# Interleaving the gate and up accumulations of a feed-forward pair, matmul by matmul, in a float32 two-block kernel

## Chip, cores and metric

The kernel runs on one NeuronCore of a Trainium2 chip. The metric is the time of one execution on the device in microseconds, as the median of several runs; lower is better.

## What is computed

Two residual blocks follow each other on 512 tokens of width 1024, all in float32. Each block is a half-weighted feed-forward, a mixer and a second half-weighted feed-forward. The mixer of the first block is a retention with a pooled branch, that of the second a gated delta rule with a short convolution. Most of the arithmetic is in the four feed-forwards:

```python
D_MODEL, SEQ, D_FF = 1024, 512, 2816

def rmsnorm(x, g):
    xf = x.astype(jnp.float32)
    y = xf * lax.rsqrt(jnp.mean(xf * xf, axis=-1, keepdims=True) + NORM_EPS)
    return (y * g.astype(jnp.float32)).astype(x.dtype)

def swiglu_ffn(x, w_in, w_out):
    gate, up = jnp.split(x @ w_in, 2, axis=-1)
    return (jax.nn.silu(gate) * up) @ w_out

# in each block
h = h + 0.5 * swiglu_ffn(rmsnorm(h, norm_ffn1), ffn1_w_in, ffn1_w_out)
...
h = h + 0.5 * swiglu_ffn(rmsnorm(h, norm_ffn2), ffn2_w_in, ffn2_w_out)
```

## The kernel before, in words

Activations lie transposed, with the channels on the 128 partitions and the 512 tokens along the free dimension. A row of 128 channels is one tile of 128x512; the residual has KD = 8 rows, the inner width of a feed-forward KF = 22.

Every float32 operand of a large product is split into two parts, `hi` and `lo` for activations, `wh` and `wl` for weights (`split_into`, L200: ScalarE writes the high part at L202, then VectorE the rest at L203). A product is then three matmuls (`mm3`, L217): `wh` with `hi` (L218), `wh` with `lo` (L219), `wl` with `hi` (L220). All three add to one PSUM tile.

A tile of weights is loaded and split by `weights` (L208): SyncE starts a DMA into a raw tile `wr`, ScalarE makes `wh` from it and VectorE `wl`. Each of the three kinds has three buffers, used in turn: weight tile number i takes the buffers of tile i-3.

`projs` (L226) multiplies the rows `xs` with some weight tiles, each into a PSUM tile `ps` of its own with the tag `mm`. In the feed-forward (`ffn`, L348) it is called once for each of the 22 pairs f: weight tile 2f gives the gate, 2f+1 the up part. It takes the 8 rows of x for the gate (24 matmuls), then the 8 rows for the up part (24 matmuls). The `late` form, used for f = 0, does the last row of x after the others; `steps` are pieces of the norm that are run between. After the matmuls of pair f come, in the program, the steps that empty pair f-1: VectorE multiplies the gate sums with the norm's scale (L363), ScalarE applies SiLU (L364), VectorE scales the up sums (L366), multiplies both (L368), and the product is split again. There are six PSUM buffers, so three pairs. After the pairs the same helper `weights` feeds the second product with `w_out`, 66 matmuls into one PSUM tile for each of 8 output rows.

`projs` with two weight tiles is also called in the first mixer (L503) for the two halves of the query and of the key of each of four heads.

The instructions of an engine stand in a fixed order, which a scheduler chooses when the kernel is built. It starts from the order of the program and moves an instruction back where, by its own reckoning of times, its inputs come later than those of others.

Of the kernel before, what the change touches and what calls it, by code (L numbers as in the profile page):

```python
# [16 lines left out]
P = 128  # L17
T = 512
NT = T // P
D = 1024  # L20
# [3 lines left out]
EPS = 1e-6  # L24
# [3 lines left out]
SB = 16  # L28
# [35 lines left out]
def shape_constants():  # L64
    """Tables that follow from the shapes alone."""
    c = np.zeros((P, NCONST), np.float32)
# [43 lines left out]
class Steps:  # L110
    """A generator that is run a step at a time, and what it returns."""

# [32 lines left out]
def tile_blocks(ctx: ExitStack, tc: tile.TileContext, ins, out, stop=None):  # L145
    nc = tc.nc
# [37 lines left out]

# [1 line left out]
    def tmp():  # L186
# [5 lines left out]
    def split(dst_pool, tag, bufs, src, shape=None, scale=None):  # L192
        """src = hi + lo exactly, both of the width that one pass takes."""
        shape = shape or [P, T]
        hi = dst_pool.tile(shape, F32R, name=nm("hi"), tag=tag, bufs=bufs)
        lo = dst_pool.tile(shape, F32R, name=nm("lo"), tag=tag, bufs=bufs)
        split_into(hi, lo, src, scale)
        return hi, lo
# [9 lines left out]
    def weights(src, nk, m):  # L208
        """One stage of weights: [P, nk, m] of them, split on arrival."""
        raw = wp.tile([P, nk, m], F32, name=nm("wr"), tag="wr", bufs=3)  # L210
        nc.sync.dma_start(raw, src)
        wh = wp.tile([P, nk, m], F32R, name=nm("wh"), tag="wh", bufs=3)
        wl = wp.tile([P, nk, m], F32R, name=nm("wl"), tag="wl", bufs=3)
        split_into(wh, wl, raw)
        return wh, wl
# [6 lines left out]
    def proj(psp, src, xs, bufs):  # L222
        """[P outputs, T] of the rows xs through one tile of weights."""
        return projs(psp, [src], xs, bufs)[0]

    def projs(psp, srcs, xs, bufs, steps=(), ws=None, order=None, late=False):  # L226
        """The same through some tiles of weights, a late last row after all others, with steps of something else between."""
        n = len(xs)
        ws = ws or [weights(src, n, P) for src in srcs]
        pss = [psp.tile([P, T], F32, name=nm("ps"), tag="mm", bufs=bufs) for _ in srcs]  # L230
        order = order or range(n)
        for ks in ((order[: n - 1], order[n - 1 :]) if late else (order,)):
            for (wh, wl), ps in zip(ws, pss):
                for k in ks:
                    mm3(ps, wh[:, k, :], wl[:, k, :], *xs[k], k == order[0], k == order[-1])
                if len(ks) > 1 and steps:
                    steps[0].step()
                    steps = steps[1:]
        return pss

    def rsqrt_cols(src, n, scale, eps=EPS):
        """(src * scale + eps) ** -0.5, by Newton steps."""
        v = rp.tile([P, n], F32, name=nm("rv"), tag="rv", bufs=4)
        nc.vector.tensor_scalar(v, src, scale, eps, ALU.mult, ALU.add)
        return newton(v, n)
# [15 lines left out]
    def spread(psp, cols, groups=1):  # L261
        """cols [P tokens, NT, groups] as [P, T]: each group's on its share of the partitions."""
        ps = psp.tile([P, T], F32, name=nm("pb"), tag=SM[0][0], bufs=SM[0][1])
        spread_into(ps, cols, groups)
        return ps
# [8 lines left out]
    def row_sums(psp, parts, of, tag=None):  # L274
        """-1 times the sums over the partitions that each column of `of` takes."""
        tag, bufs = tag or SM[0]
        ps = psp.tile([P, T], F32, name=nm("pr"), tag=tag, bufs=bufs)
        for j, part in enumerate(parts):
            nc.tensor.matmul(ps, of, part, start=(j == 0), stop=(j == 1))
        return ps  # L280

    def rms_rows(psp, src, sq, y, scale, eps):
        """y = (sum * scale + eps) ** -0.5 [P, T] of the sums of src over all partitions, with sq as scratch: from a logarithm, then a Newton step. In steps."""
        parts = [tp.tile([P, T], F32R, name=nm("t"), tag="t", bufs=5) for _ in range(2)]
# [13 lines left out]
    class Prep:  # L298
        """Takes the rows of the residual as they get ready: their split products with a gain,
        and the sums of their squares."""  # L300

# [28 lines left out]
        def scales(self, psp):  # L330
            """1/rms of each token, on all partitions [P, T], in steps; with a second gain also that of the
            normed row times it: 1/sqrt(s2/D + EPS (s1/D + EPS)) of the sums s1, s2 of squares."""
            (acc, sq), rest = self.last[0], self.last[1:]
# [70 lines left out]
    def last_add(d):  # L404
        """The squares of a finished row of the last residual; the row itself gets its gain."""
        sq = stmp()
# [9 lines left out]
    def last_out(psp, op, ps, cols):  # L416
        """The last row, for some tokens, and what depends on it: their norm and output."""
        d, n = KD - 1, (cols.stop - cols.start) // P
# [37 lines left out]
    def mix1(prep, nxt):  # L456
        xs = prep.xs
        w = ins["w_in"]
        with ExitStack() as c:
# [25 lines left out]
            with ExitStack() as c2:  # L485
# [11 lines left out]
                for hd in range(RH):  # L497
# [16 lines left out]
                    qs, ks = qk  # L514
                    # v with tokens on partitions
                    if hd == 0:
# [7 lines left out]
                    for t in range(NT):  # L524
# [9 lines left out]
                        if t in (1, 2) and fin:  # L534
                            fin[t + 1].step()
                    # scores of the tokens up to each chunk's end
                    offs = [0, 512, 896, 1152]
# [104 lines left out]
    def mix2(prep, nxt):  # L642
# [3 lines left out]
        with ExitStack() as c:  # L646
            yp = K.pool(c, nm("yc"))
            yc, os_ = [None] * 4, [None] * GH
            with ExitStack() as c2:
# [46 lines left out]
                def tok_sums(s, n, rhs):  # L696
                    """Sums over partitions of a tile [P, T], as columns [P tokens, NT, n]."""
                    ps = bank([P, NT, n])
# [10 lines left out]

                # b and a, a token per partition  # L710
                sc = Steps(prep.scales(psp))
# [15 lines left out]
                def decays():  # L727
                    """beta and the decays of all heads."""
                    yield LAG["d0"]
# [15 lines left out]
                    nc.vector.tensor_tensor(th(z), ba[:, :, 4:8], hb(vcol("gdn_dt_bias_2", 0, 4)), ALU.add)  # L745
                    # softplus(z) = max(z, 0) + log(1 + e), e = exp(-|z|); log(1 + e) = 2 atanh(e / (2 + e))
                    e_, s_, s2, a_ = ct(16), ct(16), ct(16), ct(16)
# [13 lines left out]
                    yield LAG["d2"]  # L761
                    # sums within a chunk, its last one, and the decays
                    pg = bank([P, 16])
# [26 lines left out]
                def conv(x_, names, i, kw):  # L790
                    """Causal convolution over the tokens of a tile of channels."""
                    nt = 12 if kw == 4 else 4
# [18 lines left out]
                def settle():  # L811
                    """What awaits the last row: the norm, and the rest of b and a."""
                    nonlocal rb
                    ba_rows(range(KD))
                    rb, = sc.result()
                    shorts.append(Steps(decays()))

                def chain(hd, q, k, v):
                    gl, er, dec = decay(hd)
                    bh, egh, gdh = (th(x)[:, :, hd] for x in (beta, eg, gd))  # L820
                    # k and v with tokens on partitions
                    pk = bank()
# [17 lines left out]
                    yield LAG["c1"]  # L840
                    # 1/|k| as columns
                    irk, es = ct(4), ct(4)
# [19 lines left out]
                    yield LAG["c5"]  # L862
                    # the inverse of a unit triangle: blocks of SB by substitution, with the rows of each
                    # block on all its partitions, then two doublings
                    c32 = ep.tile([P, NT, 2 * SB], F32, name=nm("c32"), tag="c32", bufs=2)
# [69 lines left out]
                    yield LAG["c10"]  # L935
                    # the recurrence over chunks, from a state of zeros
                    st = gp.tile([P, P], F32, name=nm("st"), tag="st", bufs=2)
                    po = psp.tile([P, T], F32, name=nm("po"), tag="o", bufs=1)
                    for ci in range(NCH):
# [29 lines left out]
                        yield LAG["r1"]  # L969
                    # the norm of the output, with that of q in it  # L970
                    so = stmp()
# [66 lines left out]
                def tick():  # L1038
                    """After a pass of the projections: one step of what is due, its LAG of passes after the last."""
                    tick.n += 1  # L1040
# [25 lines left out]

# [1 line left out]
    def dump():  # L1068
# [47 lines left out]

# [1 line left out]
def _tiles(w):  # L1118
    """[K, N] as [N/P, P, K/P * P]: each tile of output columns in one run per partition."""
    k, n = w.shape  # L1120
# [5 lines left out]
def _cols(v):  # L1126
    """[..., n * P] as [P, ... * n]."""
    return np.asarray(v).reshape(-1, P).T
# [62 lines left out]
```

## Time and profile before

| | |
|---|---|
| median of 3 runs | 2309.75 us (2309.1 to 2310.97) |
| span of the profiled execution | 2307.3 us |
| the median less that span | 2.45 us |
| TensorE busy | 2272.6 us, 98% of the span |
| weight loads (beside matmuls) | 1863.1 us |
| VectorE busy | 1137.0 us, 49% |
| ScalarE busy | 810.3 us, 35% |
| mean granted TensorE clock | 0.995 of full speed |

No time of the profiled execution as a whole is listed beside its span; the runs' median is 2.45 us above the span, which is taken as what lies around it. TensorE's busy time adds up overlapping matmuls, whose ends are modelled; how fast it goes is read from the distance between the starts of successive matmuls. Idle time of an engine that is not the bottleneck costs nothing.

### The profile page before, as it was taken

How to read it: one execution, taken by the hardware profiler on the slowest of the kernel's cores; microseconds unless marked ns; L12 is line 12 of the kernel's file. 1: busy time of each engine (PE TensorE's matmuls, PEld its weight loads, DVE VectorE, ACT ScalarE, POOL GpSimd, SP SyncE). 2: the span in 40 equal slices, each digit the busy share in tenths (PEclk: the TensorE clock that was granted, in tenths of full speed). 3: DMA queues.
4: the chain of work that ended last, by engine and by line, in shares of the span. 5: the costliest groups of instructions: out<-in, count | busy, mean ns of one | idle time of the engine just before them, and what ended most of it. 6: DMA issues, size and time to landing. Idle time of an engine off the chain costs nothing. (4 is left out here: it accounts for less than half of the span.)

```text
span 2307.3 us, 25697 instructions
## 1 busy us (share of the span) xinstructions
PE 2272.6 (98%) x10476; PEld 1863.1 (81%) x10476; DVE 1137.0 (49%) x1703; ACT 810.3 (35%) x1059; POOL 76.3 (3%) x78
## 2 busy tenths in 40 slices
PE   8999999999999999999999999999999999999998
PEld 6888888888878888888888888887777778888887
DVE  6444434665553444444336444334867655444332
ACT  5232223444432234233235332223534344233221
POOL 1000000000210000000000000000111000000000
PEclk9999999999999999999999999999999999999999
DMA  4333333222233333333333333333211123323332
GB/s 158 92 100 100 92 93 108 87 87 83 74 100 101 91 99 99 99 94 98 94 91 95 98 99 96 90 99 93 65 46 37 47 58 98 101 91 101 94 94 69
DMA packets 61190, 208.34 MB, mean 90 GB/s; under 512 B 6800, under 2 KB 9232, under 8 KB 61072
## 3 DMA queue, kind: packets, MB, share of 16 engines
q1 hardware_dynamic: 58544, 203.48, 28.9%
q10 hardware_dynamic: 2528, 3.21, 0.4%
q8 instruction: 82, 1.34, 0.2%
q14 instruction: 36, 0.29, 0.0%
HBM read 204.57 MB, written 2.10 MB: 90 GB/s over the span
## 5 line engine op out<-in xcount | busy, mean ns | idle before, releaser
L218 PE MATMUL ps<-hi,wh 128*128 128x512 f32 (+1 forms) x2774 | 1082.8, 391 | 6.4 <-ACT wh L202 6.4
L219 PE MATMUL ps<-lo,wh 128*128 128x512 f32 (+1 forms) x2774 | 1082.4, 390 | 0.8 <-DVE lo L206 0.8
L220 PE MATMUL ps<-hi,wl 128*128 128x512 f32 (+1 forms) x2774 | 1082.3, 390 | 0.6 <-DVE wl L203 0.6
L202 ACT ACTIVATE wh<-wr 128x1024 fp32r<-128x1024 f32 (+1 forms) x390 | 406.3, 1042 | 1159.6 <-PE ps L219 630.8
L203 DVE TENSOR_TENSOR wl<-wr,wh 128x1024 fp32r<-128x1024 f32 (+1 forms) x390 | 470.2, 1206 | 341.1 <-ACT wh L202 340.8
L218 PEld LDWEIGHTS ps<-hi,wh 128*128 128x128 f32 x2774 | 521.9, 188 | 119.5 <-ACT wh L202 6.4
L219 PEld LDWEIGHTS ps<-lo,wh 128*128 128x128 f32 x2774 | 521.5, 188 | 115.7 <-DVE lo L206 3.2
L220 PEld LDWEIGHTS ps<-hi,wl 128*128 128x128 f32 x2774 | 521.5, 188 | 114.9 <-DVE wl L203 2.5
L366 DVE TENSOR_TENSOR t<-ps,rb 128x512 f32<-128x512 f32 x88 | 60.7, 690 | 258.6 <-PE ps L220 258.6
L363 DVE TENSOR_TENSOR t<-ps,rb 128x512 f32<-128x512 f32 x88 | 60.8, 690 | 169.9 <-PE ps L220 169.8
L202 ACT ACTIVATE hi<-t 128x512 fp32r<-128x512 f32 x119 | 75.2, 632 | 112.2 <-DVE t L368 62.0
L807 PE MATMUL ps<-hi,wh 128*128 128x512 f32 x224 | 94.4, 422 | 0.4 <-DVE t L1001 0.4
L807 PE MATMUL ps<-hi,wl 128*128 128x512 f32 x224 | 93.3, 416 | 0.0
L807 PE MATMUL ps<-lo,wh 128*128 128x512 f32 x224 | 92.6, 413 | 0.0
L203 DVE TENSOR_TENSOR lo<-t,hi 128x512 fp32r<-128x512 f32 x119 | 83.3, 700 | 5.4 <-ACT hi L202 5.1
L368 DVE TENSOR_TENSOR t<-t,t 128x512 f32<-128x512 f32 x88 | 60.8, 691 | 8.2
L364 ACT ACTIVATE t<-t 128x512 f32<-128x512 f32 x88 | 54.2, 616 | 3.4 <-DVE t L363 3.3
L377 DVE SCALAR_TENSOR_TENSOR h<-ps,h 128x512 f32<-128x512 f32 x31 | 21.4, 691 | 64.4 <-PE ps L220 64.4
L807 PEld LDWEIGHTS ps<-hi,wh 128*128 128x128 f32 x224 | 42.9, 191 | 8.2 <-issue 1.0
L807 PEld LDWEIGHTS ps<-hi,wl 128*128 128x128 f32 x224 | 42.4, 189 | 8.3 <-issue 0.9
L807 PEld LDWEIGHTS ps<-lo,wh 128*128 128x128 f32 x224 | 43.1, 192 | 6.9 <-issue 0.2
L530 PE MATMUL pv<-wh,hi 128*128 128x256 f32 x128 | 36.3, 284 | 0.0
(292 smaller groups left out, 1362.1 us busy)
## 6 DMA issues: line engine op xcount, KB each, us to landing
wr<-in_ffn_w_in SPq DMA_DIRECT2D x176, 512.0 KB, 3.5
wr<-in_ffn_w_out SPq DMA_DIRECT2D x64, 512.0 KB, 3.6
wr<-in_w_in SPq DMA_DIRECT2D x48, 512.0 KB, 3.5
wr<-in_w_mix_in SPq DMA_DIRECT2D x28, 512.0 KB, 3.5
wr<-in_ffn_w_out SPq DMA_DIRECT2D x32, 384.0 KB, 3.1
wr<-in_w_v SPq DMA_DIRECT2D x8, 512.0 KB, 3.8
wr<-in_w_ret_up SPq DMA_DIRECT2D x8, 512.0 KB, 3.4
wr<-in_w_pool_up SPq DMA_DIRECT2D x8, 512.0 KB, 3.5
```

The costliest lines, as they stand in the source:

```text
L202: nc.scalar.activation(hi, src, AF.Copy)
L203: nc.vector.tensor_tensor(lo, src, hi.bitcast(F32), ALU.subtract)
L218: nc.tensor.matmul(ps, lh, rh, start=start, stop=False)
L219: nc.tensor.matmul(ps, lh, rl, start=False, stop=False)
L220: nc.tensor.matmul(ps, ll, rh, start=False, stop=stop)
L363: nc.vector.tensor_tensor(g, pg, rb, ALU.mult)
L364: nc.scalar.activation(g, g, AF.Silu)
L366: nc.vector.tensor_tensor(u, pu, rb, ALU.mult)
L368: nc.vector.tensor_tensor(m, g, u, ALU.mult)
L377: nc.vector.scalar_tensor_tensor(h[d], ps, 0.5, h[d], ALU.mult, ALU.add)
L530: nc.tensor.matmul(pv, xh[:, sl], wh[:, k % 4, :], start=(k == 0), stop=False)
L807: nc.tensor.matmul(ps, a[:, k, :], b, start=(k == j == 0), stop=(k == KD - 1 and j == 2))
```

## The change

Where `projs` has more than one weight tile, no late row and no steps, it now goes through the rows k of x, for each through the three kinds of matmul, and for each of these through the weight tiles: gate and up alternate. The matmuls of such pairs have line 237; later lines are 7 higher (L363 is L370, L366 is L373, L368 is L375). The rest of the diff takes out comments and docstrings.

```diff
         order = order or range(n)
+        if len(pss) > 1 and not late and not steps:
+            for k in order:
+                for j in range(3):
+                    for (wh, wl), ps in zip(ws, pss):
+                        a = (wh, wh, wl)[j][:, k, :]
+                        nc.tensor.matmul(ps, a, xs[k][j == 1], start=(k == order[0] and j == 0), stop=(k == order[-1] and j == 2))
+            return pss
         for ks in ((order[: n - 1], order[n - 1 :]) if late else (order,)):
             for (wh, wl), ps in zip(ws, pss):
                 for k in ks:
```

The form applies to 83 pairs of the feed-forwards (all but f = 0 of each, and f = 1 of the first, which has steps) and to the key pair of each of the four heads. The number of matmuls is the same.

TensorE, in the first feed-forward, before: the end of the gate and the start of the up part of one pair. ps_984 and ps_985 are the gate and up sums of the pair, wh_974 and wl_975 the gate's weights, wh_980 and wl_981 the up part's; hi and lo are rows of x.

```order
L218 MATMUL ps_984<-hi_146,wh_974 128x512
L219 MATMUL ps_984<-lo_147,wh_974 128x512
L220 MATMUL ps_984<-hi_146,wl_975 128x512
L218 MATMUL ps_985<-hi_105,wh_980 128x512 [waits Activation_49]
L219 MATMUL ps_985<-lo_106,wh_980 128x512
L220 MATMUL ps_985<-hi_105,wl_981 128x512 [waits DVE_49]
```

The last use of the gate's wh_974 stands 25 matmuls before the pair's end.

TensorE, the same place in the changed kernel: the end of that pair, and then the start of the next one, whose sums are ps_1057 and ps_1058, with wh_1047 and wl_1048 for the gate and wh_1053 and wl_1054 for the up part. wh_1053 and wl_1054 take the buffers of wh_974 and wl_975.

```order
L237 MATMUL ps_984<-lo_147,wh_974 128x512
L237 MATMUL ps_985<-lo_147,wh_980 128x512
L237 MATMUL ps_984<-hi_146,wl_975 128x512
L237 MATMUL ps_985<-hi_146,wl_981 128x512
L237 MATMUL ps_1057<-hi_105,wh_1047 128x512 [waits Activation_49]
L237 MATMUL ps_1057<-lo_106,wh_1047 128x512
L237 MATMUL ps_1057<-hi_105,wl_1048 128x512 [waits DVE_49]
L237 MATMUL ps_1058<-hi_105,wh_1053 128x512 [waits Activation_49]
L237 MATMUL ps_1058<-lo_106,wh_1053 128x512
```

```order
L237 MATMUL ps_1057<-hi_110,wh_1047 128x512
L237 MATMUL ps_1057<-lo_111,wh_1047 128x512
L237 MATMUL ps_1057<-hi_110,wl_1048 128x512
L237 MATMUL ps_1058<-hi_105,wl_1054 128x512 [waits DVE_49]
L237 MATMUL ps_1058<-hi_110,wh_1053 128x512
```

The second fence follows directly on the first. The scheduler has moved the first up matmuls back by a few places; from the 13th matmul of a pair on, gate and up alternate strictly. The last use of wh_974 now stands 7 matmuls before the first use of wh_1053 and 12 before the first use of wl_1054.

VectorE around the same pair, in the changed kernel: the emptying of the gate sums ps_984 (L370) and of the up sums ps_985 (L373), with the weights' low parts between.

```order
L370 TENSOR_TENSOR t_1107<-ps_984,rb_267 128x512 [waits PE_49]
L203 TENSOR_TENSOR wl_1054<-wr_1051,wh_1053 128x1024 [waits DMAHW3_49,Activation_49]
L373 TENSOR_TENSOR t_1110<-ps_985,rb_267 128x512 [waits PE_49]
L203 TENSOR_TENSOR wl_1121<-wr_1118,wh_1120 128x1024 [waits DMAHW4_49,Activation_49]
L375 TENSOR_TENSOR t_1112<-t_1107,t_1110 128x512 [waits DVE_49,Activation_49]
```

Before, the order of the first three was the same, and wl_1121 stood behind the product L368. On ScalarE wh_1053 stands behind the previous pair's steps as before, and wh_1120 now directly behind it.

## Rows read from the trace of the kernel before

**Rows 1.** The page: the span, and two lines of its 40 slices in tenths.
```profile
span 2307.3 us, 25697 instructions
PE   8999999999999999999999999999999999999998
PEclk9999999999999999999999999999999999999999
```

**Rows 2.** Timeline of TensorE, 100 to 124 us: start us, us, engine, line, operation.
```profile
99.73 0.39 PE L218 MATMUL ps<-hi,wh 128*128 128x512 f32 x1
99.96 0.39 PE L219 MATMUL ps<-lo,wh 128*128 128x512 f32 x1
100.19 0.39 PE L220 MATMUL ps<-hi,wl 128*128 128x512 f32 x1
100.42 0.39 PE L218 MATMUL ps<-hi,wh 128*128 128x512 f32 x1
...
105.40 0.39 PE L219 MATMUL ps<-lo,wh 128*128 128x512 f32 x1
105.63 0.39 PE L220 MATMUL ps<-hi,wl 128*128 128x512 f32 x1
...
123.99 0.39 PE L220 MATMUL ps<-hi,wl 128*128 128x512 f32 x1
```

**Rows 3.** Timeline of VectorE, 100 to 124 us; in brackets the idle time before.
```profile
100.61 0.69 DVE L366 TENSOR_TENSOR t<-ps,rb 128x512 f32<-128x512 f32 x1 [3.30 <-PE ps L220]
101.41 0.69 DVE L368 TENSOR_TENSOR t<-t,t 128x512 f32<-128x512 f32 x1
102.02 1.22 DVE L203 TENSOR_TENSOR wl<-wr,wh 128x1024 fp32r<-128x1024 f32 x1
...
106.06 0.69 DVE L363 TENSOR_TENSOR t<-ps,rb 128x512 f32<-128x512 f32 x1 [2.21 <-PE ps L220]
106.97 1.22 DVE L203 TENSOR_TENSOR wl<-wr,wh 128x1024 fp32r<-128x1024 f32 x1 [0.23 <-ACT wh L202]
```

**Rows 4.** Timeline of ScalarE, 100 to 124 us.
```profile
105.88 1.06 ACT L202 ACTIVATE wh<-wr 128x1024 fp32r<-128x1024 f32 x1 [3.11 <-PE ps L219]
```

**Rows 5.** Timeline of TensorE, product with w_out, 299.7 to 311.9 us: first and last.
```profile
299.40 0.40 PE L220 MATMUL ps<-hi,wl 128*128 128x512 f32 x1
...
311.77 0.40 PE L219 MATMUL ps<-lo,wh 128*128 128x512 f32 x1
```

**Rows 6.** Timelines of ScalarE and of weight loads, start of the kernel: TensorE's wait.
```profile
5.30 1.06 ACT L202 ACTIVATE wh<-wr 128x1024 fp32r<-128x1024 f32 x1 [0.67 <-DMA wr<-in_ffn_w_in]
...
6.40 0.29 PEld L218 LDWEIGHTS ps<-hi,wh 128*128 128x128 f32 x1 [6.40 <-ACT wh L202]
```

**Rows 7.** Timeline of all engines, 656 to 660 us: a wait of TensorE on VectorE.
```profile
655.92 0.69 DVE L203 TENSOR_TENSOR lo<-t,hi 128x512 fp32r<-128x512 f32 x1 [0.70 <-ACT hi L202]
...
656.67 0.19 PEld L219 LDWEIGHTS pm<-lo,wh 128*128 128x128 f32 x1 [0.54 <-DVE lo L203]
...
656.78 0.19 PEld L220 LDWEIGHTS pm<-hi,wl 128*128 128x128 f32 x1
...
659.07 0.50 PE L218 MATMUL pm<-hi,wh 128*128 128x512 f32 x1 [1.66 <-DVE lo L206]
```

**Rows 8.** Timeline of TensorE, matmuls of 256 columns, 404.7 to 407.9 us: first and last.
```profile
404.51 0.28 PE L530 MATMUL pv<-wh,hi 128*128 128x256 f32 x1
...
407.87 0.28 PE L531 MATMUL pv<-wl,hi 128*128 128x256 f32 x1
```

**Rows 9.** Timeline of TensorE, 1660.6 to 1664.2 us, in the second mixer.
```profile
1661.09 0.63 PE L807 MATMUL ps<-hi,wh 128*128 128x512 f32 x1
1661.52 1.91 PE L271 MATMUL pg<-cst,c 128*128 128x128 f32 x8
```

**Rows 10.** Stretches: PE, PEld, DVE, ACT, POOL busy (instructions), granted clock, DMA share, GB/s.
```profile
650.00:660.00 10.00, 8.12 (x34) 5.91 (x33) 8.07 (x12) 4.02 (x6) 2.17 (x2) 1.00 0.44 113
...
1661.00:1664.00 3.00, 3.00 (x15) 2.81 (x13) 2.69 (x7) 2.88 (x6) 0.00 (x0) 0.50 0.35 78
```

## The prediction

> **What bounds the kernel now.** I read the page first: TensorE has no slice below 0.8 and full clock in all 40 [rows 1]. So time is matmuls times the distance of their starts, plus gaps. The next view is the timeline of TensorE inside a feed-forward. From 99.73 to 123.99 us there are 107 distances in 24.26 us, 0.2267 us each, with no gap [rows 2]. A pair of 48 takes 10.88 us.
>
> The same view answers the change's question, since it holds a change of bank every 24 matmuls. The matmul at 100.19 is the last of an up part: VectorE starts to empty it at 100.61 [rows 3]. The next, at 100.42, is the first of a gate, in another bank. Their distance is 0.23; the 24 distances from 100.19 to 105.63, this one among them, average 0.2267, and the 23 without it 0.2265 [rows 2]. A switch of bank gains nothing that can be seen. Nor does it matter whether successive matmuls share weights: L218 to L219 does, L219 to L220 does not, and both distances are 0.23.
>
> Then the timelines of ScalarE and VectorE for what prepares weights. The split of a tile starts when the last matmul that reads the buffer's former tile is done: L219 at 105.40, ScalarE at 105.88, 0.48 later [rows 2, 4]. VectorE's part starts 1.09 after ScalarE's and takes 1.22 [rows 3, 4]. Before the change that is far ahead of need: the up part's buffers come free in the middle of a pair, and 24 matmuls (5.4 us) pass before the pair ends.
>
> **The change, part by part.** *Same count of matmuls, loads and DMAs.* Nothing is added; bank switches rise from 2 to 40 in a pair (counted in the order of the changed kernel), for 87 pairs. Price of a switch: 0, by the distance at 100.42.
>
> *The same x row in two successive matmuls.* The trace has no such pair. Its nearest rows are the two distances that it shows for other operands, 0.2267 in the pairs and 12.37 us over 53, 0.2334, in the product with w_out [rows 2, 5]. Bounds: 0.0067 more for some 20 such successions in 87 pairs, 12 us; below, a gain down to the fixed part worked out under the rivals. I take 0, since operands and buffers are those of the 0.2267 rows.
>
> *Weights needed sooner and released later.* This is the term that counts. The gate's `wh` is now read up to the 45th matmul of its pair, and its buffer is what the next pair's up weights wait for. In the changed order the next up part first reads `wh` 7 matmuls after that release matmul and `wl` 12 after it. Counted from the start of the release matmul:
>
> - due: `wh` at 7 x 0.2267 = 1.587 us, `wl` at 12 x 0.2267 = 2.72 us;
> - `wh` ready: 0.48 (release to ScalarE) + 1.06 (its duration [rows 4]) + 0.04 (6.36 to 6.40, its end to the weight load [rows 6]) = 1.58 us;
> - `wl` ready: 0.48 + 1.09 + 1.22 + 0.06 (656.61 to 656.67 [rows 7]) = 2.85 us;
> - after a wait the weight load is no longer hidden: the next load follows 0.11 after the first (656.67 to 656.78 [rows 7]). So the matmuls run at 1.69 and 2.96.
>
> `wh` is 0.10 late, and `wl` 0.24 late in all (the first delay is inside it). VectorE must be free: its gate evacuation stands directly ahead of `wl`. It starts 0.43 after its last matmul (105.63 to 106.06 [rows 2, 3]), which is two after the release: 0.45 + 0.43 = 0.88. The next operation can follow 0.61 later (101.41 to 102.02 [rows 3]), at 1.49, before `wh` is done at 1.57. So it hides, by 0.08 us; with the 0.80 between L366 and L368 [rows 3] instead of 0.61 it would add 0.11.
>
> Sum: of the 83 interleaved pairs 80 stand behind a pair that releases late. In 77 the distances are 7 and 12; in three the scheduler put `wl` later, and 0.10 is left. 77 x 0.24 + 3 x 0.10 = 18.8 us. The four key pairs delay the value weights that follow: in three heads due at 12 x 0.12 + 4 x 0.2267 = 2.35 (`wh`) and 3 x 0.12 more, 2.71 (`wl`), so 0.25 late each, 0.75 us. Together 19.5 us.
>
> *Nothing else is late.* The raw tile of an up part is loaded a pair ahead. The later gate evacuation has three pairs of PSUM buffers and ends its chain before the next pair needs anything. At the end of a feed-forward the last row of the inner product is needed only 65 matmuls on. Cover lost: none beyond the weights.
>
> On the profiled execution's own time: 2307.3 + 19.5 = 2326.8 us of span, and with the 2.45 us around it **2329 us**, 0.8% above the median of 2309.75. Bounds of this case: if only the `wh` delay remains, 80 x 0.10 = 8 us (2318); if evacuation adds 0.11 and successive equal rows cost their 12 us, 19.5 + 8.5 + 12 = 40 us (2350). The links of the chain each carry 0.02 to 0.05 us, small against 2.85 but not against 0.24.
>
> **Rivals.**
>
> *The waits vanish.* The chain misses by 0.24 of 2.96 us; were the weight load after a wait hidden after all and one link 0.13 shorter, the time would stay at 2309.8. Against it: every link is from a row. This also covers the change not doing what it says, since the first 12 matmuls of a pair hardly alternate. Chance 0.08.
>
> *Banks pay, the other side.* Matmuls of 256 columns start 3.36 / 28 = 0.120 us apart [rows 8], those of 512 columns 0.2267. So 256 columns cost 0.1067, and 0.0133 us is fixed for each matmul. If that fixed part belonged to writing the same bank twice, 38 more switches in 87 pairs would give back 38 x 87 x 0.0133 = 44 us: 2329 - 44 = **2285 us**, faster. It decides from 0.006 us a switch on, where it outweighs 19.5. Against it: the switch at 100.42 shows none of it. For it: a switch to a bank's first matmul overwrites, and a switch back to a running sum is not in the trace. Chance 0.06.
>
> The Trainium skill, "Perfetto Trace Analysis", section "Matmuls", wants independent groups to rotate through PSUM banks so that emptying one overlaps the next, and says nothing of single matmuls; the kernel before rotates in that way already, and VectorE's rows show the emptying beside matmuls, so by that rule nothing is gained here.
>
> *An evacuation in front.* If gate and up evacuation both came ahead of `wl` in time, or the gate's came one operation late, `wl` waits 0.61 more: 0.85 x 77 = 65 us, **2376 us**. For it: VectorE works in order, and the margin is 0.08 us. Against it: the printed order has only one there. Chance 0.06.
>
> *The clock falls.* TensorE now pauses at each pair. In a stretch with a granted clock of 0.50 (the level of 1.2 GHz) the next matmul started 0.43 us after one of 512 columns (1661.09 to 1661.52 [rows 9, 10]); if half of the 3984 matmuls of the pairs ran so, 1992 x 0.20 = 400 us, **2730 us**. Against it: around 657 us TensorE waited 1.66 us at once, and the granted clock of that stretch stayed 1.00 [rows 7, 10]; the new pauses are a tenth of that. Chance 0.02.
>
> The Trainium skill, "TensorE: Matmul & The Clock Gate", section "A second HAM failure mode: psum-queue depth-cycling", reports a kernel that cycled through PSUM banks, paused briefly between groups and lost its clock again and again. By that rule this change would end in the clock rival; the rows above speak against it here.
>
> **How the numbers follow.** The forecast has 0.78, waits vanishing 0.08, banks 0.06, an evacuation 0.06, the clock 0.02. The range takes the forecast's own bounds, 2318 to 2350, and reaches down to the unchanged time, 2308, which leaves out some 0.17. A measurement of this kernel can tell 0.2%, 4.6 us, from no change. Faster: 0.06 (banks). Same: 0.08. Slower: 0.78 + 0.06 + 0.02 = 0.86.
>
> **What would show it.** Right: in a pair the 36 alternating matmuls stay 0.2267 apart; the first up matmul waits on ScalarE's `wh`, and more often the first with `wl` on VectorE's `wl`; pairs last 11.1 us; ScalarE's idle time before `wh` ends on matmuls of L237 shortly before a pair's end; clock as before; w_out unchanged at 0.2334. Wrong: distances of 0.22 or less between alternating matmuls (banks pay), distances of 0.23 and more throughout (equal rows cost), no wait at all at the start of pairs, or waits of half a microsecond and more (evacuation in front).

## The result and the profile after

The changed kernel takes 2332.28 us (median of 4 runs, 2331.19 to 2333.24) against 2309.76 us before (4 runs). The ratio is 1.0096, 95% interval 1.0082 to 1.011: slower by 22.5 us. Forecast were 2329 us within 2308 to 2350.

The page of the changed kernel, its head and four of its costliest groups (columns: line, engine, operation, count | busy us, mean ns | idle us just before them and what ended most of it):

```profile
span 2331.5 us, 25691 instructions
...
PE 2295.1 (98%) x10476; PEld 1850.0 (79%) x10476; DVE 1129.5 (48%) x1703; ACT 800.6 (34%) x1059; POOL 76.1 (3%) x78
...
PEclk9999999999999999999999999999999999999999
...
L202 ACT ACTIVATE wh<-wr 128x1024 fp32r<-128x1024 f32 (+1 forms) x390 | 396.5, 1038 | 1072.1 <-PE ps L237 464.9
...
L237 PE MATMUL ps<-hi,wl 128*128 128x512 f32 x1392 | 453.3, 396 | 1.0 <-DVE wl L203 1.0
L237 PEld LDWEIGHTS ps<-hi,wl 128*128 128x128 f32 x1392 | 261.1, 188 | 75.3 <-DVE wl L203 22.2
L237 PEld LDWEIGHTS ps<-hi,wh 128*128 128x128 f32 x1392 | 261.2, 188 | 71.3 <-ACT wh L202 21.1
```

The span is 24.2 us longer than in [rows 1], at the same clock in all 40 slices, and TensorE's share is 98% as before. The page's matmul rows show almost no idle time; a reader who looks there alone would find nothing. The weight loads (PEld) tell it: 22.2 us of idle time ended by VectorE's `wl` and 21.1 us ended by ScalarE's `wh`. ScalarE's own idle time now ends on matmuls of L237: it stands still until a pair's last matmuls give the buffer back.

How often, from the chain of waits of the changed kernel, weight loads only, 60 to 240 us (engine, tile, line, what it waited for: us in total, times, longest):

```profile
PEld ps L237 <- DVE wl L203: 4.3, 16, 0.3
PEld ps L237 <- ACT wh L202: 4.2, 16, 0.3
```

The stretch holds 16.1 pairs, so each pair has both waits once. In the kernel before the same view of the same stretch has no wait of a weight load at all.

One pair's border in the changed kernel, from the timelines of the four engines (start us, us, engine, line, operation; "x2" are two instructions in one line, the second 0.23 after the first):

```profile
100.25 0.62 PE L237 MATMUL ps<-hi,wh 128*128 128x512 f32 x2
100.70 0.61 PE L237 MATMUL ps<-lo,wh 128*128 128x512 f32 x2
...
102.06 0.39 PE L237 MATMUL ps<-hi,wl 128*128 128x512 f32 x1
102.29 0.50 PE L237 MATMUL ps<-hi,wh 128*128 128x512 f32 x1
102.63 0.39 PE L237 MATMUL ps<-lo,wh 128*128 128x512 f32 x1
...
103.33 0.72 PE L237 MATMUL ps<-hi,wl 128*128 128x512 f32 x2
103.89 0.40 PE L237 MATMUL ps<-hi,wh 128*128 128x512 f32 x1
...
105.98 0.62 PE L237 MATMUL ps<-hi,wh 128*128 128x512 f32 x2
...
111.42 0.62 PE L237 MATMUL ps<-hi,wh 128*128 128x512 f32 x2
...
112.78 0.39 PE L237 MATMUL ps<-hi,wh 128*128 128x512 f32 x1
```

```profile
101.18 2.01 ACT L202 ACTIVATE wh<-wr 128x1024 fp32r<-128x1024 f32 x2 [5.84 <-PE ps L237]
```

```profile
101.58 0.69 DVE L370 TENSOR_TENSOR t<-ps,rb 128x512 f32<-128x512 f32 x1 [5.52 <-PE ps L237]
102.27 1.23 DVE L203 TENSOR_TENSOR wl<-wr,wh 128x1024 fp32r<-128x1024 f32 x1
```

```profile
101.84 0.19 PEld L237 LDWEIGHTS ps<-hi,wl 128*128 128x128 f32 x1
102.29 0.19 PEld L237 LDWEIGHTS ps<-hi,wh 128*128 128x128 f32 x1 [0.27 <-ACT wh L202]
102.40 0.19 PEld L237 LDWEIGHTS ps<-lo,wh 128*128 128x128 f32 x1
...
103.55 0.19 PEld L237 LDWEIGHTS ps<-hi,wl 128*128 128x128 f32 x1 [0.27 <-DVE wl L203]
```

The matmul at 100.70 is the last that reads the gate's `wh`. ScalarE starts 0.48 later, VectorE's `wl` 1.09 after ScalarE, and the two weight loads that need them start at 102.29 and 103.55, 1.59 and 2.85 after the release. A load usually starts with the matmul before its own, as the one at 101.84 does; these start one matmul later. The cost of each wait is read from the matmuls: 102.29 to 102.63 is 0.34 instead of 0.23, and from 103.33 two distances take 0.56 instead of 0.45. So 0.11 each, 0.22 for both. A third part is small and was not forecast: from 102.63 to 103.33 three distances take 0.70 instead of 0.68, and from 103.89 to 105.98 nine take 2.09 instead of 2.04. Behind a wait some matmuls run at about 0.233 before the old distance is back. From 105.98 to 112.78 it is: 30 distances in 6.80 us, 0.2267 each, gate and up alternating.

One pair, 100.25 to 111.42, takes 11.17 us instead of 10.88. Over the stretch from 60 to 240 us the recorded starts give, for a pair of 48, 0.215 us in distances above 0.25 (two of them) and 0.069 us in some twelve distances between 0.228 and 0.25: 0.284 in all. Times 77 pairs this is 21.9 us of the 24.2 by which the span grew. Counted over the interleaved stretches of all four feed-forwards, the loss is 23.4 us: most of what is beyond 21.9 is one longer wait, 1.4 us, at the start of the third feed-forward, which skew3 below has as well. That the span grew by more than the median is a matter of single executions: the profiled one of the changed kernel, 2333.24 us, is the slowest of its four.

### The profile page after: what moved, and what is told of

Its sections match the earlier page's. It is cut to its first block, busy times and chain, and to the rows that moved or that the text cites. A ratio compares the mean times of both kernels' runs of the same rounds, so it can differ in the third digit from the quotient of the medians.

```text
span 2331.5 us, 25691 instructions
## 1 busy us (share of the span) xinstructions
PE 2295.1 (98%) x10476; PEld 1850.0 (79%) x10476; DVE 1129.5 (48%) x1703; ACT 800.6 (34%) x1059; POOL 76.1 (3%) x78
## 5 line engine op out<-in xcount | busy, mean ns | idle before, releaser
L202 ACT ACTIVATE wh<-wr 128x1024 fp32r<-128x1024 f32 (+1 forms) x390 | 396.5, 1038 | 1072.1 <-PE ps L237 464.9
L218 PE MATMUL ps<-hi,wh 128*128 128x512 f32 (+1 forms) x1382 | 541.4, 392 | 6.6 <-ACT wh L202 6.6
L219 PE MATMUL ps<-lo,wh 128*128 128x512 f32 (+1 forms) x1382 | 540.9, 391 | 0.6 <-DVE lo L206 0.5
L220 PE MATMUL ps<-hi,wl 128*128 128x512 f32 (+1 forms) x1382 | 540.8, 391 | 0.6 <-DVE wl L203 0.6
L237 PE MATMUL ps<-hi,wh 128*128 128x512 f32 x1392 | 466.6, 396 | 0.1
L237 PE MATMUL ps<-lo,wh 128*128 128x512 f32 x1392 | 459.0, 390 | 0.0
L237 PE MATMUL ps<-hi,wl 128*128 128x512 f32 x1392 | 453.3, 396 | 1.0 <-DVE wl L203 1.0
L237 PEld LDWEIGHTS ps<-hi,wl 128*128 128x128 f32 x1392 | 261.1, 188 | 75.3 <-DVE wl L203 22.2
L237 PEld LDWEIGHTS ps<-hi,wh 128*128 128x128 f32 x1392 | 261.2, 188 | 71.3 <-ACT wh L202 21.1
L218 PEld LDWEIGHTS ps<-hi,wh 128*128 128x128 f32 x1382 | 260.9, 189 | 64.9 <-ACT wh L202 6.6
L219 PEld LDWEIGHTS ps<-lo,wh 128*128 128x128 f32 x1382 | 260.4, 188 | 61.3 <-DVE lo L206 3.0
L220 PEld LDWEIGHTS ps<-hi,wl 128*128 128x128 f32 x1382 | 260.2, 188 | 60.4 <-DVE wl L203 2.1
L237 PEld LDWEIGHTS ps<-lo,wh 128*128 128x128 f32 x1392 | 261.4, 188 | 52.0
L370 DVE TENSOR_TENSOR t<-ps,rb 128x512 f32<-128x512 f32 x88 | 60.8, 691 | 434.6 <-PE ps L237 434.5
L814 PE MATMUL ps<-hi,wh 128*128 128x512 f32 x224 | 94.1, 420 | 0.4 <-DVE t L1008 0.4
L814 PE MATMUL ps<-hi,wl 128*128 128x512 f32 x224 | 93.4, 417 | 0.0
L814 PE MATMUL ps<-lo,wh 128*128 128x512 f32 x224 | 92.3, 412 | 0.0
L375 DVE TENSOR_TENSOR t<-t,t 128x512 f32<-128x512 f32 x88 | 60.2, 684 | 0.3
L373 DVE TENSOR_TENSOR t<-ps,rb 128x512 f32<-128x512 f32 x88 | 60.1, 682 | 0.0
```

Source lines behind the costliest of these rows:

```text
L202: nc.scalar.activation(hi, src, AF.Copy)
L218: nc.tensor.matmul(ps, lh, rh, start=start, stop=False)
L219: nc.tensor.matmul(ps, lh, rl, start=False, stop=False)
L220: nc.tensor.matmul(ps, ll, rh, start=False, stop=stop)
L237: nc.tensor.matmul(ps, a, xs[k][j == 1], start=(k == order[0] and j == 0), stop=(k == order[-1] and j == 2))
L370: nc.vector.tensor_tensor(g, pg, rb, ALU.mult)
```

## The experiments

All were timed beside the kernel before, whose medians were 2309.28, 2309.73 and 2309.16 us in the three groups of runs.

| run | median us | ratio to before, 95% interval |
|---|---|---|
| skew3: alternating, gate three ahead | 2310.7 | 1.0006 (0.9997 to 1.0015) |
| skew2: alternating, gate two ahead | 2315.76 | 1.0024 (1.0014 to 1.0033) |
| byrow: alternating by rows of x | 2324.62 | 1.0064 (1.0052 to 1.0077) |
| inter_wh4: changed, 4 `wh`, 2 raw tiles | 2342.78 | 1.0147 (1.0131 to 1.0162) |
| plain_wh4: before, 4 `wh`, 2 raw tiles | 2316.3 | 1.0027 (1.0016 to 1.0038) |
| inter_wl4: changed, 4 `wl`, 2 raw tiles | 2331.2 | 1.0093 (1.0078 to 1.0108) |
| plain_pad: before, padding behind the rows | 2291.5 | 0.9922 (0.9908 to 0.9935) |
| plain_padw: before, padding ahead of the weights | 2342.19 | 1.014 (1.0125 to 1.0155) |
| plain_pad0: padding in both places | 2290.9 | 0.9921 (0.9904 to 0.9938) |
| inter_pad: changed, padding behind the rows | 2313.87 | 1.0018 (1.0009 to 1.0028) |

### Alternating without late weights

The gate keeps alternating with the up part, but starts three matmuls ahead and ends three ahead. Its buffers come free earlier and the up part's weights are needed later.

```diff
-            for k in order:
-                for j in range(3):
-                    for (wh, wl), ps in zip(ws, pss):
+            seq = [(k, j) for k in order for j in range(3)]
+            for t in range(len(seq) + 3):
+                for i, ((wh, wl), ps) in enumerate(zip(ws, pss)):
+                    if 0 <= t - 3 * i < len(seq):
+                        k, j = seq[t - 3 * i]
```

> Gate and up still alternate matmul by matmul and change the PSUM bank at nearly every one, but the gate runs three matmuls ahead: it ends three earlier, and the up part starts three later. The up part's first wh then stands 11 matmuls (2.49 us) after the last reader of its buffer and its first wl 15 (3.40 us), against 1.69 and 2.96 us that the chain of refilling takes. Late-weights theory: no wait at the start of a pair, 2310 to 2312 us. Banks-pay rival: without the waits the gain of alternating stands alone, 44 us below the kernel before, about 2266 us, and clearly below 2300 if only half of it is real. Rival that alternating itself costs (the row of x read twice, the bank switches): 2325 us and more, with no waits.

Measured: 2310.7 us, the time of before within what can be told. The stretch 60 to 240 us of this kernel, from the table of stretches (busy us and instructions of PE, PEld, DVE, ACT, POOL, then granted clock, DMA share, GB/s):

```profile
60.00:240.00 180.00, 180.00 (x796) 149.05 (x795) 80.08 (x98) 53.02 (x65) 0.00 (x0) 1.00 0.32 98
```

and of the changed kernel:

```profile
60.00:240.00 180.00, 180.00 (x776) 142.78 (x775) 80.31 (x98) 50.70 (x65) 0.00 (x0) 1.00 0.31 96
```

The one has 796 matmuls in 180 us (0.2267 apart by their starts) and no wait of a weight load; the other has 20 fewer. Nearly every matmul of the first writes another bank than the one before it. So by its interval the alternation alone gains at most 0.03% and costs at most 0.15% (3.5 us), and the rest of the 22.5 us is the price of the late weights.

### The size of the margin

The same with the gate two ahead:

```diff
-            for t in range(len(seq) + 3):
+            for t in range(len(seq) + 2):
...
-                    if 0 <= t - 3 * i < len(seq):
-                        k, j = seq[t - 3 * i]
+                    if 0 <= t - 2 * i < len(seq):
+                        k, j = seq[t - 2 * i]
```

> As skew3, with the gate two matmuls ahead instead of three: 9 matmuls to the first use of wh and 13 to that of wl. Chain theory with the links of the prediction: wh due at 9 x 0.2267 = 2.04 us against 1.58, wl at 13 x 0.2267 = 2.95 against 2.85; both in time, the second by 0.10, so 2309 to 2312. If the chain is longer than read by over 0.10 us, each pair waits 0.11 for wl and runs some matmuls slower after it: 2318 to 2321.

Measured: 2315.76 us, between the two numbers. Timelines of TensorE, of the weight loads and of VectorE in this kernel:

```profile
99.32 0.39 PE L239 MATMUL ps<-lo,wh 128*128 128x512 f32 x1
...
101.82 0.61 PE L239 MATMUL ps<-lo,wh 128*128 128x512 f32 x2
102.27 0.64 PE L239 MATMUL ps<-hi,wl 128*128 128x512 f32 x2
102.75 0.62 PE L239 MATMUL ps<-hi,wh 128*128 128x512 f32 x2
103.21 0.62 PE L239 MATMUL ps<-lo,wh 128*128 128x512 f32 x2
```

```profile
100.89 1.22 DVE L203 TENSOR_TENSOR wl<-wr,wh 128x1024 fp32r<-128x1024 f32 x1
```

```profile
102.17 0.30 PEld L239 LDWEIGHTS ps<-hi,wl 128*128 128x128 f32 x2 [0.16 <-DVE wl L203]
```

The chain has the forecast's length to 0.01: release at 99.32, load at 102.17, 2.85 later. The expectation compared this with the start of the matmul (2.95) and left out that a load starts ahead of its matmul, usually by a whole matmul, which would be 2.72 here. So the load is late by a part of a matmul only, 0.13. Its own matmul at 102.27 is on time (0.45 after the pair at 101.82), but the following take 0.48 and 0.46 for two instead of 0.453. The recorded starts of the stretch from 60 to 240 us give 0.053 us for a pair, 0.042 of it in six distances of 0.228 to 0.25: some 4 us for 77 pairs, of the 6 measured. A weight load that is late without delaying its own matmul is not free.

### Emptying in front of the weights

Gate and up alternate by rows of x, three matmuls each:

```diff
             for k in order:
-                for j in range(3):
-                    for (wh, wl), ps in zip(ws, pss):
-                        a = (wh, wh, wl)[j][:, k, :]
-                        nc.tensor.matmul(ps, a, xs[k][j == 1], start=(k == order[0] and j == 0), stop=(k == order[-1] and j == 2))
+                for (wh, wl), ps in zip(ws, pss):
+                    mm3(ps, wh[:, k, :], wl[:, k, :], *xs[k], k == order[0], k == order[-1])
```

> Gate and up alternate by rows of x, three matmuls each, so the bank changes at every third. The buffers come free one matmul earlier than in the changed kernel: wh is due 8 matmuls (1.81 us) after the last reader, above the 1.69 us of its chain. On VectorE both evacuations now stand ahead of the up part's wl. Late-weights theory with VectorE in order: no wait on ScalarE's wh; wl starts only after the up evacuation, at 0.91 + 0.43 + 0.61 = 1.95 us after the last reader, and is ready at 3.33 us with the exposed weight load against 3.17 us due: 0.16 us late in some 77 pairs, 12 to 15 us with the slower matmuls after each wait, about 2323 us. Theory of the buffers alone (evacuations never matter): wl ready at 2.96 us against 3.17 due, no wait, 2311 us. Banks-pay rival: a third of the 44 us back.

Measured: 2324.62 us, as the theory with VectorE's order had it. Timelines of VectorE and of ScalarE at a pair's border of this kernel:

```profile
100.72 0.69 DVE L368 TENSOR_TENSOR t<-ps,rb 128x512 f32<-128x512 f32 x1 [6.21 <-PE ps L220]
101.40 0.69 DVE L371 TENSOR_TENSOR t<-ps,rb 128x512 f32<-128x512 f32 x1
102.01 1.22 DVE L203 TENSOR_TENSOR wl<-wr,wh 128x1024 fp32r<-128x1024 f32 x1
```

```profile
100.55 2.01 ACT L202 ACTIVATE wh<-wr 128x1024 fp32r<-128x1024 f32 x2 [7.10 <-PE ps L219]
```

Both emptyings stand ahead of `wl`, which starts 1.46 after ScalarE instead of 1.09: 0.37 us later. This is the rival "an evacuation in front" made on purpose. The wait on `wh` is gone here, that on `wl` is left once a pair (16 times in the 16 pairs from 60 to 240 us).

### Which buffer is short

A fourth buffer for `wh` (with one raw tile less, so that the buffers take no more memory):

```diff
-        raw = wp.tile([P, nk, m], F32, name=nm("wr"), tag="wr", bufs=3)
+        raw = wp.tile([P, nk, m], F32, name=nm("wr"), tag="wr", bufs=2)
...
-        wh = wp.tile([P, nk, m], F32R, name=nm("wh"), tag="wh", bufs=3)
+        wh = wp.tile([P, nk, m], F32R, name=nm("wh"), tag="wh", bufs=4)
```

> The changed kernel with four buffers for wh and two for the raw weights. The up part's wh no longer waits for the pair before it; its wl still takes the buffer of the gate's wl, whose last reader is the 47th matmul of the pair before, and is due 7 matmuls (1.59 us) later in the new order. Chain: 0.43 (to VectorE, no evacuation ahead in this order) + 1.22 + 0.06 + 0.11 = 1.82 us. Late-weights theory: one wait in a pair in place of two, on VectorE's wl, 0.23 us and the slower matmuls after one wait: about 2329 us, almost as slow as the changed kernel although a buffer was added. Rival that the wait on wh carries the cost: half of it gone, 2320 us or less.

Measured: 2342.78 us, some 14 us above what was expected. In the trace the wait on `wh` is gone, as it should be, but the wait on `wl` is longer. Timelines of VectorE, weight loads and TensorE:

```profile
101.76 1.22 DVE L203 TENSOR_TENSOR wl<-wr,wh 128x1024 fp32r<-128x1024 f32 x1 [5.64 <-PE ps L237]
```

```profile
103.03 0.19 PEld L237 LDWEIGHTS ps<-hi,wl 128*128 128x128 f32 x1 [0.44 <-DVE wl L203]
```

```profile
101.28 0.62 PE L237 MATMUL ps<-hi,wl 128*128 128x512 f32 x2
...
102.64 0.90 PE L237 MATMUL ps<-hi,wl 128*128 128x512 f32 x2
103.37 0.62 PE L237 MATMUL ps<-hi,wh 128*128 128x512 f32 x2
```

With `wh` in time the scheduler no longer holds the up part's first matmuls back: gate and up alternate from the first matmul on. The up part's `wl` is then needed 7 matmuls after the last use of the buffer's former tile (101.28), and VectorE now waits for that matmul itself. The same links give 0.48 + 1.22 + 0.06 = 1.76 us to the load, 0.11 more to the matmul, against 7 x 0.2267 = 1.59: 0.28 late, and 102.64 to 103.37 is 0.73 instead of 0.45, which is 0.28. With the slower matmuls behind it a pair loses 0.31 us by the recorded starts, 24 us in 77 pairs. One buffer was replaced by the next as the short one, at a worse distance.

The same buffers in the order of before:

> Control for the run with four wh buffers: the order of before, two raw tiles instead of three, four wh and three wl. If the extra 10 us that inter_wh4 took over the chain's sum come from the third raw tile that it gave up (a tile's DMA then starts only when wl of the tile two before is done), this kernel is slower than before by about as much, 2318 to 2322. If two raw tiles cost nothing in the pairs and the mixers, it stays at 2309 to 2311, and inter_wh4's rest has to be in its pairs.

Measured: 2316.3 us, 6.6 us above before and between the two numbers expected. Its pairs keep their distance (795 matmuls from 60 to 240 us, no wait of a load), but ScalarE now waits for DMAs, a line that the same view of before does not have (chain of waits, 60 to 240 us):

```profile
ACT wh L202 <- DMA wr<-in_ffn_w_in: 23.5, 10, 2.5
```

In the trace the loss arises in the mixers: 3.2 us by the starts of the matmuls around one wait in the first (658 to 664 us, where the granted clock is 0.56, against 1.00 in the kernel before), the rest in the second. Whether the waits for DMAs bring this about is not shown. If the 6.6 us carry over to the changed order, 2309.3 + 24 + 6.6 = 2340 of the 2342.8 are accounted for; the next run speaks against calling them the price of the raw tile.

A fourth buffer for `wl` instead, again with two raw tiles:

> The changed kernel with two raw tiles, three wh and four wl. Chain theory: the short buffer is wh, since VectorE's wl starts when ScalarE's wh ends and not when its own buffer comes free; the 7 and 12 matmuls from the release of wh stay, so both waits of a pair stay: about 2332, plus what two raw tiles cost in plain_wh4. Rival: wl waits for its own buffer, which is read to the pair's last matmul; then the wl wait goes and only that on wh is left: 80 x 0.11 and some slower matmuls behind each, 2318 to 2322, plus the same.

Measured: 2331.2 us, the time of the changed kernel, so the price expected for two raw tiles did not appear (from 60 to 240 us ScalarE waits for no DMA here). Both waits are there in every pair:

```profile
PEld ps L237 <- DVE wl L203: 4.3, 16, 0.3
PEld ps L237 <- ACT wh L202: 4.2, 16, 0.3
```

`wl` is late because it is made from a late `wh`, not for want of its own buffer. A fourth buffer for both kinds was not tried.

### The other distance, 0.2334

The forecast left open why the product with `w_out` runs at 0.2334 [rows 5] and the pairs at 0.2267. In the built kernel the tiles of weights and of the rows of x start at 32 modulo 64 bytes of a partition, the inner rows of the product with `w_out` at 0 (the layout of the build; the traces hold no addresses). Adding 32 bytes behind the pool of the norm's rows moves all later pools to 32:

```diff
     rp = K.pool(ctx, "rows")
+    padp = K.pool(ctx, "pad")
+    padt = padp.tile([P, 8], F32, name="padt")
+    nc.vector.memset(padt, 0.0)
```

> The kernel before with 32 bytes of padding in each partition ahead of the pools that hold the inner products and the mixers' rows, and one small memset. In the kernel before matmuls start 0.2267 us apart where the rows come from the pool of x (its tiles start at 32 modulo 64 bytes, as the weights' do) and 0.2333 us where they come from pools whose tiles start at 0 modulo 64. Theory that this distance follows from the two addresses: after the shift the product with w_out runs at 0.2267 too; some 2900 matmuls times 0.0067 us, 19 us less, about 2291 us. Rival that the distance belongs to the stage (44 rows in place of 8, longer accumulations): 2310 us.

Measured: 2291.5 us, faster than both kernels. Then the same lines ahead of the pool `wts` instead, which leaves rows of x at 32 and moves the weights to 0 and later rows to 32; and plain_pad with the same lines a second time ahead of the pool `xsplit`, which puts all at 0.

> Before, with 32 bytes of padding ahead of the pool of the weights instead of behind it: weights move from 32 to 0 modulo 64 bytes, rows of x stay at 32, and the rows of every later pool move from 0 to 32. If the start of the moving rows alone sets the distance of matmuls (32 good, 0 bad), all products run at 0.2267 and the time is that of plain_pad, about 2291. If the two operands have to stand alike modulo 64, all are now unlike: the pairs' 48 x 88 and the other matmuls on rows of x run at 0.2333 instead of 0.2267, 6048 of them (fewer count, those of 256 columns by less): 2309 + some 25 to 40 us, 2334 to 2349.

> plain_pad with 32 more bytes ahead of the rows of x too: rows of x, weights and the rows of all later pools stand at 0 modulo 64 bytes. If rows and weights only have to stand alike, all products run at 0.2267 as in plain_pad: about 2291. If both have to stand at 32, all run at 0.2333 as in plain_padw: about 2342.

Measured: 2342.19 and 2290.9 us. The table of stretches shows it by counting matmuls in a pair stretch (60 to 240 us) and in one of `w_out` (310 to 380 us). The kernel before:

```profile
60.00:240.00 180.00, 180.00 (x796) 149.10 (x795) 82.82 (x99) 53.99 (x66) 0.00 (x0) 1.00 0.32 97
310.00:380.00 70.00, 70.00 (x302) 56.44 (x301) 25.68 (x29) 20.61 (x25) 0.00 (x0) 1.00 0.35 101
```

plain_pad, rows and weights at 32 everywhere:

```profile
60.00:240.00 180.00, 180.00 (x796) 149.05 (x795) 82.95 (x99) 54.03 (x66) 0.00 (x0) 1.00 0.31 97
310.00:380.00 70.00, 70.00 (x311) 57.96 (x310) 26.11 (x30) 20.98 (x25) 0.00 (x0) 1.00 0.38 113
```

plain_padw, rows at 32 and weights at 0 everywhere:

```profile
60.00:240.00 180.00, 180.00 (x773) 144.92 (x772) 81.43 (x98) 52.80 (x65) 0.00 (x0) 1.00 0.31 94
310.00:380.00 70.00, 70.00 (x301) 56.35 (x300) 22.78 (x26) 18.99 (x22) 0.00 (x0) 1.00 0.31 93
```

plain_pad0, rows and weights at 0 everywhere:

```profile
60.00:240.00 180.00, 180.00 (x796) 149.05 (x795) 82.73 (x99) 54.01 (x66) 0.00 (x0) 1.00 0.32 97
310.00:380.00 70.00, 70.00 (x310) 57.98 (x309) 25.92 (x30) 21.00 (x25) 0.00 (x0) 1.00 0.38 114
```

Where the two operands stand alike modulo 64, a stretch of 70 us holds 310 or 311 matmuls and one of 180 us 796; where they stand unlike, 301 or 302, and 773. Neither 0 nor 32 is better by itself. The changed kernel has 302 in its `w_out` stretch, as before; this effect has no part in its loss, which the last run shows from the other side:

> The changed kernel with plain_pad's 32 bytes behind the pool of rows. The waits of the pairs and the distance of the other products have nothing to do with each other, so the two differences add: 2332.3 - 17.8 = 2314.5, say 2312 to 2317; the pairs show the same two waits of 0.11 us. If the pairs' waits came from the later stages' distance in any way, the sum would be off by more than 3 us.

Measured: 2313.87 us. The two effects add to within 0.6 us (2332.28 - 17.78 = 2314.50), and the fastest of all kernels here is plain_pad or plain_pad0 (their intervals overlap), both without the interleaving.

## Why the prediction was right

**TensorE as the bound; same work.** Right: same counts of matmuls and loads, same clock, TensorE at 98%. The 2.45 us "around" the span are not all around it: where a run's time and span are both known they differ by 1.7 to 2.1 us, and the rest is that the profiled execution was faster than the median. The sum, which forecasts a median, is not hurt.

**Bank switches at price 0.** Right. In the changed kernel 30 alternating distances average 0.2267, and skew3 with alternating banks comes to 1.0006 (0.9997 to 1.0015) of before. The rival "banks pay" wanted 44 us less.

**The same row of x twice at price 0.** Right: the same 30 distances hold such successions. The upper bound of 12 us was not used up.

**Weights needed sooner and released later.** Right, and the cause of the loss: 0.48 to ScalarE, 1.09 to VectorE, loads 1.59 and 2.85 after the release against the forecast's 1.58 and 2.85. skew3, which takes away the lateness and leaves the alternation, gives the time back; inter_wl4, which adds buffers where they were not short, does not; inter_wh4 moves the short place and its 0.28 follows from the same links. The count was right too: the whole trace has 80 waits on `wh` and 78 on `wl`, one of them the longer one of the third feed-forward; forecast were 80 and 77. The key pairs cost 0.2 us in each of three heads, forecast were 0.25.

**The step that was mis-sized** is the sum for a pair, "late 0.24 in all". The waits cost 0.10 forecast and 0.11 measured for `wh`, 0.14 forecast and 0.11 measured for `wl`. Left out was that matmuls behind a wait run slower for a while: 0.07 us a pair. Those between the two waits also make the second a little later due, so the second costs less than forecast. Together 0.284 instead of 0.24, 3.4 us in 77 pairs, which is what separates 2332.3 from 2329.

**Emptying hidden by 0.08.** Right, the margin included. The emptying starts at 101.58, 0.88 after the release as worked out. In each of the 16 pairs from 60 to 240 us `wl` starts 0.03 after the end of `wh` (here 101.18 + 1.06 = 102.24, and 102.27), as in the kernel before, where VectorE stood idle in front of `wl` (105.88 + 1.06 = 106.94, and 106.97 [rows 3, 4]). Where the emptying ends last, as in byrow, `wl` starts 0.61 after the emptying's start (101.40 to 102.01); here it starts 0.69 after it. So `wh` ends last, by 0.08. byrow shows the price when it is the emptying: `wl` starts 0.37 us later.

**The clock rival** fell: the granted clock of 60 to 240 us is 1.00 with 32 short waits in it. The row that the prediction set against it was weaker than it looked. The same wait of 1.66 us in the first mixer, behind which the kernel before kept a granted clock of 1.00 (659 to 663 us), is followed in the changed kernel by matmuls 0.43 us apart, a part of a stretch at 1.2 GHz (a row of the timeline of TensorE, and one of the table of stretches):

```profile
664.91 0.79 PE L218 MATMUL pm<-hi,wh 128*128 128x512 f32 x1 [1.66 <-DVE lo L206]
...
664.00:668.00 4.00, 3.09 (x7) 2.48 (x8) 2.17 (x4) 0.92 (x2) 0.00 (x0) 0.58 0.39 131
```

So one wait after which the clock stayed did not show that such a wait is harmless, and that this argument came out right is in part luck; what shows that the pairs' short waits are harmless to the clock is their own stretch. The mean granted clock is 0.995 in both profiled executions, so the clock has no share in the loss that could be told. The Trainium skill, "TensorE: Matmul & The Clock Gate", section "A second HAM failure mode: psum-queue depth-cycling", reports a clock lost again and again by a kernel that cycled through PSUM banks and paused briefly between groups of matmuls. The pairs of this study do not show it, with 0.11 us at a time.

**The waits vanish**: they did not in the changed kernel, and did in skew3, where 11 and 15 matmuls lie between the release and the first uses.

## What to carry to other kernels

Before reordering matmuls, count the matmuls from the last use of a buffer's old tile to the first use of its new one, and compare with the time of the whole refill, each link taken from the timeline; interleaving two accumulations lengthens the life of both weight tiles and brings the uses nearer, and here 7 and 12 matmuls were too few while 11 and 15 cost nothing. Look for the loss at the weight loads, since the matmul rows may show no idle time, and count what follows a wait too. Where like matmuls run at two distances in one kernel, compare where their operands start in memory: 32 bytes of padding took 18 us off this one.

## What was not expected of the hardware

**Alike starts.** float32 matmuls of 512 columns start 0.2267 us apart when the moving rows and the weights start alike modulo 64 bytes (32 and 32, or 0 and 0), 0.2333 when one is at 0 and the other at 32. On this kernel that is 18 us saved (plain_pad, 0.9922) or 33 us lost (plain_padw, 1.014). Why it is so the runs don't show, and other offsets than 0 and 32 were not tried.

**Slower matmuls behind a wait.** After a weight load that waited, several matmuls start 0.229 to 0.240 us apart before 0.2267 returns: about 12 a pair in the changed kernel with its two waits, 4 in inter_wh4 with one, and 6 in skew2, where the load's own matmul was not late. What ends these stretches stays open.
